# Keys loaded once and queries exchanged on VectorE, in the second attention of an fp32 encoder layer

## The chip, the cores and the metric

The kernel runs on one core of a Trainium2 chip. Its time is the device time of one execution in microseconds (us). Of the kernel before, three runs took 2575.32 to 2576.74 us, with a median of 2575.82 us.

The core has five engines that each run their own instructions in order: TensorE (PE, matmuls), VectorE (DVE), ScalarE (ACT), GpSimd (POOL) and SyncE (SP), which here issues most transfers (DMAs). On-chip memory (SBUF) has 128 partitions; matmuls write to PSUM.

## The reference

One layer of an encoder on 2048 tokens of width 1024, all in float32:

```
h  = rms_norm(x)
z  = h @ W_in            # q_A k_A v_A | q_B k_B v_B | gate_A | gate_B
yA = windowed GQA, |t-s| <= 128, ALiBi, a sink logit per head       (8 heads, 2 kv heads, width 64)
yB = 2-D neighbourhood attention on a 32 x 64 grid of tokens, 8 x 16 keys per query,
     with a learned bias per head and relative position             (8 heads, width 64)
x  = x + (sigmoid(gate_A) * (yA @ Wp_A) + sigmoid(gate_B) * (yB @ Wp_B)) @ W_out
x  = x + relu(rms_norm(x) @ W_up)^2 @ W_down
out = rms_norm(x)
```

## The kernel before, in words

**Precision.** PE multiplies a float32 number as a high and a low part (type fp32r). A product is three matmuls: high by high, high by low, low by high. In the two attentions one operand of 64 rows (a head's width) leaves half of the 128 partitions free, so high and low parts lie on the two halves of the partitions: rows 0 to 63 and rows 64 to 127. One matmul over 128 partitions then gives two of the products, and a second one with the halves of one operand exchanged gives the others.

**Stages.** In the order of PE: the in-projection's first part (0 to about 360 us); the first attention (windowed, class `Unit`, to about 612 us); the second attention (neighbourhood, class `Near`, to about 908 us); the late gates, the projections of the attentions' outputs, and the two MLP products. Both attentions are interleaved with dense matmuls of the in-projection (lines L205 to L207, drawn from a generator by `plain()`), so that PE has work while softmaxes run. Constants (`STEP`, `SCORE`) spread the dense matmuls over the attention's chunks; `in_turn()` ties each of PE's groups behind the one before.

**One unit of the first attention.** 128 queries of four heads. Scores (L846, PE), addition of a bias and maximum (L850, DVE), exponential (L865, ACT), shares, that is the division by the sum (L871, POOL), transposes (L906), the high part (ACT) and low part (DVE) of the transposed shares, the product with v (L931, PE). For the outer keys of a unit, 64-row pieces of v are copied to the tile `ve` (L887, POOL, method `rows`), in one buffer.

**One unit of the second attention.** There are 32 units: 8 heads times 4 column blocks. Scores (L1118): for each of four row groups two matmuls, z = 0 and 1, with the same queries `qb` and with the keys `kb` plain and with halves exchanged. Then bias and maximum (L1125, DVE, a custom operation), exponential (L1138, ACT), the reciprocal of the sum (L1142, DVE), shares (L1145, POOL, `weigh`), transposes (L1157, PE, `turn`), high part `phb` (L1165, ACT), low part `plb` (L1166, DVE), product with v (L1178, PE), sum of the two halves (L1197 and L1198). A loop over "doubles" (half a unit each) makes the transposes of unit n, the scores of unit n + 2 and the loads of unit n + 3.

**Loads of the second attention.** `load_k(h)` loads a head's keys three times over, as `[P, 2, S]`: all 128 rows (1 MB), and the two exchanged halves (0.5 MB each); from the second head on most of them are issued from ACT's queue. `Near.load` loads the queries of a unit (256 KB) and makes its bias: `make_bias_b` (L1070, L1076) loads a table `braw` by DMA and adds the mask to it in three operations on POOL, for three of four column blocks.

**Placement.** The tiles of an attention lie in SBUF in the order of two lists (`ap_` for the first, `bp` for the second). A new tile waits until the old tiles whose bytes it overlaps are done with. The late stage's weights (`graw`) come into the space of the second attention's tiles.

## Time and profile before

| what | value |
|---|---|
| median of 3 runs | 2575.82 us (2575.32 to 2576.74) |
| the profiled execution's own time | 2576.89 us |
| its span, first to last instruction | 2575.1 us |
| granted clock of TensorE, mean | 0.999 |
| busy: PE, DVE, ACT, POOL | 2544.6, 1655.4, 1247.0, 385.3 us |
| transfers | 494.61 MB, 192 GB/s over the span |

The profile's page gives the busy time of each engine. A timeline row gives the start, the length, the engine, the line, the operation with its output and inputs, how many instructions it stands for, and in brackets the engine's idle time just before it and what ended it. A row of waits gives the engine and its line, the releaser, the microseconds in all, how often, and the longest. A row of a stretch gives its length and the busy time of each engine in it.

### The profile page before, as it was taken

Reading aid. Unit: us, or ns where it says so; the run is one execution under the profiler, and the core shown is the slowest. Engines: PE = TensorE matmul, PEld = TensorE weight load, DVE = VectorE, ACT = ScalarE, POOL = GpSimd, SP = SyncE. Lnnn points to the kernel's source line nnn. Section 1 sums busy time; section 2 is a strip of 40 time slices with the busy share of each in tenths; the row PEclk is TensorE's granted clock in tenths of the full one; section 3 lists DMA queues with packets and bytes.
Section 4 is the critical chain, followed back from the end, with each engine's and each line's share of the span. In section 5 each row is a group of like instructions: output and inputs, shape, how many; then the busy total and the mean of one; then the engine's idle time right before and its main releaser. Section 6 shows DMA issues by size and latency. Waiting matters only on the chain.

```text
span 2575.1 us, 34947 instructions
## 1 busy us (share of the span) xinstructions
PE 2544.6 (99%) x12152; PEld 2131.9 (83%) x12152; DVE 1655.4 (64%) x2691; ACT 1247.0 (48%) x2283; POOL 385.3 (15%) x622
## 2 busy tenths in 40 slices
PE   8999999999999999999999999999999999999998
PEld 6888888888899888888888888888888888888887
DVE  8776657765565576565568767865666534554766
ACT  5344347776666654443335554554444322323454
POOL 1000126665666400000000000100000000000010
PEclk9999999999999999999999999999999999999999
DMA  5667486577898647576447656844428725444555
GB/s 181 200 165 202 134 263 170 130 194 191 227 245 215 200 149 261 184 229 184 122 161 252 236 199 219 304 160 163 147 111 315 273 103 188 144 156 155 187 194 174
DMA packets 350225, 494.61 MB, mean 192 GB/s; under 512 B 29000, under 2 KB 180808, under 8 KB 347872
## 3 DMA queue, kind: packets, MB, share of 16 engines
q1 hardware_dynamic: 343312, 465.90, 57.2%
q10 hardware_dynamic: 6736, 26.48, 3.4%
q8 instruction: 96, 1.57, 0.3%
q14 instruction: 81, 0.66, 0.1%
HBM read 332.83 MB, written 159.45 MB: 191 GB/s over the span
## 4 chain that ended last, share of the span: by engine, by line
PE 86%; DMA 2%; DVE 1%; POOL 1%; issue 0%; ACT 0%; POOLq 0%; ACTq 0%; DVEq 0%
PE b L318 16%; PE b L319 16%; PE b L320 16%; PE mm L205 5%; PE mm L207 5%; PE mm L206 5%; PE pt L205 2%; PE pt L206 2%; PE pt L207 2%; PE av L1178 2%; PE pt L1157 2%; PE s L1118 2%; PE av L931 1%; PE s L846 1%; PE pt L906 1%; PE zb L318 1%
## 5 line engine op out<-in xcount | busy, mean ns | idle before, releaser
L319 PE MATMUL b<-dwh,dah 128*128 128x512 f32 x896 | 348.9, 389 | 0.0
L320 PE MATMUL b<-dwh,dah 128*128 128x512 f32 x896 | 347.9, 389 | 0.0
L318 PE MATMUL b<-dwh,dah 128*128 128x512 f32 x896 | 339.9, 389 | 0.0
L314 ACT CAST dah<-da 128x1024 fp32r<-128x1024 f32 (+1 forms) x128 | 120.7, 944 | 367.7 <-PE b L320 244.2
L315 DVE TENSOR_TENSOR dah<-da,dah 128x1024 fp32r<-128x1024 f32 (+1 forms) x128 | 139.6, 1090 | 224.9 <-ACT dah L314 222.0
L319 PE MATMUL b<-ubh,uwhlb 128*128 128x512 f32 x592 | 230.5, 389 | 0.0
L318 PE MATMUL b<-ubh,uwhlb 128*128 128x512 f32 x592 | 230.4, 390 | 0.0
L320 PE MATMUL b<-ubh,uwhlb 128*128 128x512 f32 x592 | 229.4, 389 | 0.0
L318 PEld LDWEIGHTS b<-dwh,dah 128*128 128x128 f32 x896 | 168.3, 188 | 34.9
L319 PEld LDWEIGHTS b<-dwh,dah 128*128 128x128 f32 x896 | 168.3, 188 | 34.8
L320 PEld LDWEIGHTS b<-dwh,dah 128*128 128x128 f32 x896 | 168.3, 188 | 34.8
L318 PE MATMUL zb<-zh,zwhl 128*128 128x512 f32 x476 | 186.8, 394 | 5.0 <-DVE zc L309 1.7
L319 PE MATMUL zb<-zh,zwhl 128*128 128x512 f32 x476 | 186.0, 391 | 0.0
L320 PE MATMUL zb<-zh,zwhl 128*128 128x512 f32 x476 | 183.1, 391 | 1.8 <-DVE zwhl L315 1.8
L309 DVE TENSOR_TENSOR uc<-b,uc 128x512 f32<-128x512 f32 x160 | 109.1, 689 | 103.7 <-PE b L320 102.8
L205 PE MATMUL mm<-hT,whl 128*128 128x512 f32 x416 | 167.9, 404 | 0.7 <-DVE zc L309 0.7
L207 PE MATMUL mm<-hT,whl 128*128 128x512 f32 x416 | 163.5, 393 | 0.0
L206 PE MATMUL mm<-hT,whl 128*128 128x512 f32 x416 | 163.2, 392 | 0.0
L1876 POOL TENSOR_TENSOR st<-st,power 128x1 f32<-128x1 f32 x16 | 13.3, 841 | 925.2 <-DVE st L1875 925.2
L318 PEld LDWEIGHTS b<-ubh,uwhlb 128*128 128x128 f32 x592 | 111.2, 188 | 23.4 <-issue 0.4
L319 PEld LDWEIGHTS b<-ubh,uwhlb 128*128 128x128 f32 x592 | 111.2, 188 | 23.0
L320 PEld LDWEIGHTS b<-ubh,uwhlb 128*128 128x128 f32 x592 | 111.2, 188 | 23.0
(348 smaller groups left out, 6054.4 us busy)
## 6 DMA issues: line engine op xcount, KB each, us to landing
at<-uc SPq DMA_DIRECT2D x224, 256.0 KB
da<-at SPq DMA_DIRECT2D x96, 512.0 KB
dw<-in_w_down_dram SPq DMA_DIRECT2D x160, 256.0 KB
uraw<-in_w_up_dram SPq DMA_DIRECT2D x32, 1024.0 KB
zraw<-in_w_in_dram SPq DMA_DIRECT2D x16, 1024.0 KB
z<-zg SPq DMA_DIRECT2D x64, 256.0 KB
raw<-in_w_in_dram SPq DMA_DIRECT2D x26, 512.0 KB
zg<-zc SPq DMA_DIRECT2D x32, 256.0 KB
```

The source lines that it names most:

```text
L205: PE.matmul(ps, lh, rh, start=first, stop=False)
L206: PE.matmul(ps, lh, rl, start=False, stop=False)
L207: return PE.matmul(ps, ll, rh, start=False, stop=last).ins
L309: return eng.tensor_tensor(out=out, in0=a, in1=b, op=op).ins
L314: casts.append(A.copy(hi, src).ins)
L315: return eng.tensor_tensor(out=lo, in0=src, in1=hi.bitcast(F32), op=ALU.subtract).ins
L318: PE.matmul(ps, lh, rh, start=first, stop=False, skip_group_check=True)
L319: PE.matmul(ps, lh, rl, start=False, stop=False, skip_group_check=True)
L320: PE.matmul(ps, ll, rh, start=False, stop=last, skip_group_check=True)
L1118: ins = PE.matmul(ps[:, :n], self.q[:, i, :], kv[:, z, B_R0[i] // 4 : (B_R0[i] + B_NR[i]) // 4, 4 * B_C0[j] : 4 * (B_C0[j] + w)], start=z ...
L1157: ins = PE.transpose(pt[:kp, at + (i - i0) * P : at + (i - i0 + 1) * P], self.s[i][:, rr : rr + kp], ident).ins
L1178: issued[0] = PE.matmul(po[:, i0 * P : (i0 + ni) * P], self.v[:kp, c, :], src[:kp, o : o + ni * P], start=pair == x == z == 0, stop=(c == ...
```

## The change

Four things change together.

1. `load_k` loads a head's keys once, as `[P, S]`, in two halves along the tokens, both from SP. The tile of the queries has two versions, z = 0 plain and z = 1 with halves exchanged. The scores' two matmuls use the same keys, and the two versions of the queries.
2. The exchanged version is made on DVE by two copies of 64 rows (`swap`), except for units 0 and 1, which get it by two more DMAs each. The queries are loaded a unit earlier (`load_q`, unit n + 4 instead of n + 3).
3. The operations that make a bias are tied behind the last share that was written, or, ahead of any share of the second attention, behind chosen copies of `ve`; a unit's bias is loaded and made after `weigh` instead of first in the unit.
4. `ve` gets two buffers, and the copies for unit n + 1 are written behind the shares in unit n. In the placement, `qraw` goes to the end of its list, and `qb2` behind `biasl`.

```
-    ap_ = pools(s_a, "left", ("ka1", "va1", "qraw", "qa", "sta", "sa", "ya", "ph", "pl", "biasa1", "byhead", "ve"), "a")
+    ap_ = pools(s_a, "left", ("ka1", "va1", "qa", "sta", "sa", "ya", "ph", "pl", "biasa1", "byhead", "ve", "qraw"), "a")
...
         def rows(self):
-            self.ve = T(ap_, [P, 2, P], F32R, "ve", 1)
+            self.ve = T(ap_, [P, 2, P], F32R, "ve", 2)
...
-                        G.tensor_copy(out=self.ve[half, c // 2], in_=rows)
+                        last = G.tensor_copy(out=self.ve[half, c // 2], in_=rows).ins
+            copied_rows.append(last)
...
-        if c == "outer":
-            x.rows()
...
+        if c == "outer" and n + 1 < len(units):
+            with tc.issue_after(shares[-1]):
+                units[n + 1].rows()
...
-    bp = pools(s_b, "right", ("masks", "kb0", "qb0", "braw0", "biass0", "stb", "biass1", "qb1", "qb2", "braw1", "biasl", "kb1"), "b")
+    bp = pools(s_b, "right", ("masks", "kb0", "qb0", "braw0", "biass0", "stb", "biass1", "qb1", "braw1", "biasl", "qb2", "kb1"), "b")
...
-            G.tensor_tensor(out=out.rearrange("p (q x r) -> p q x r", x=w, r=4),
+            first_bias.append(copied_rows[min(22 + len(first_bias), 31)])
+            with tc.issue_after(last_share[0] or first_bias[-1]):
+                G.tensor_tensor(out=out.rearrange("p (q x r) -> p q x r", x=w, r=4),
...
     def load_k(h):
-        kbs[h] = k = T(bp, [P, 2, S], F32R, f"kb{h % 2}", 1)
-        kd = ks_b[h // 2][h % 2]
-        for n, (dst, src) in enumerate(((k[:, 0], kd), (k[0:64, 1], kd[64:128]), (k[64:128, 1], kd[0:64]))):
-            (SY if h == 0 or h == 1 and n == 0 else A).dma_start(dst.bitcast(F32), src)
+        kbs[h] = k = T(bp, [P, S], F32R, f"kb{h % 2}", 1)
+        for n in range(2):
+            at = slice(n * (S // 2), (n + 1) * (S // 2))
+            SY.dma_start(k[:, at].bitcast(F32), ks_b[h // 2][h % 2][:, at])
             yield
...
-            self.q = T(bp, [P, 4, P], F32R, f"qb{self.n % 3}", 1)
-            SY.dma_start(self.q.bitcast(F32), qs_b[self.h // 2][self.h % 2][:, :, self.j])
             return self.bias
+
+        def load_q(self, both=False):
+            self.q = T(bp, [P, 2, 4, P], F32R, f"qb{self.n % 3}", 1)
+            SY.dma_start(self.q[:, 0].bitcast(F32), qs_b[self.h // 2][self.h % 2][:, :, self.j])
+            for a in (0, 64) if both else ():
+                SY.dma_start(self.q[a : a + 64, 1].bitcast(F32), qs_b[self.h // 2][self.h % 2][64 - a : 128 - a, :, self.j])
+
+        def swap(self):
+            q = self.q
+            for a in (0, 64):
+                V.tensor_copy(out=q[a : a + 64, 1], in_=q[64 - a : 128 - a, 0].bitcast(F32))
...
-                    ins = PE.matmul(ps[:, :n], self.q[:, i, :],
-                                    kv[:, z, B_R0[i] // 4 : (B_R0[i] + B_NR[i]) // 4, 4 * B_C0[j] : 4 * (B_C0[j] + w)],
+                    ins = PE.matmul(ps[:, :n], self.q[:, z, i, :],
+                                    kv[:, B_R0[i] // 4 : (B_R0[i] + B_NR[i]) // 4, 4 * B_C0[j] : 4 * (B_C0[j] + w)],
...
-                G.tensor_scalar(s[i][:, :n], s[i][:, :n], ri[:, i : i + 1], 1.0, ALU.mult, ALU.mult)
+                last_share[0] = G.tensor_scalar(s[i][:, :n], s[i][:, :n], ri[:, i : i + 1], 1.0, ALU.mult, ALU.mult).ins
...
         if p == 0:
-            if n + 3 < len(units):
-                bias = units[n + 3].load(bias)
+            if n + 4 < len(units):
+                units[n + 4].load_q()
...
+        with behind_parts_b():
+            for u in (2, 3) if at == 0 else (n + 3,) if p == 0 and n + 3 < len(units) else ():
+                units[u].swap()
         if weighed:
             with behind_parts_b():
                 y, us = weighed.pop(0)
                 y.weigh(us)
+        if p == 0 and n + 3 < len(units):
+            bias = units[n + 3].load(bias)
```

The order of POOL's work at the end of the second attention's first units, before (`whl` is a low part of the dense matmuls' weights, `biass` and `biasl` are biases, `sb` shares):

```order
L1145 TENSOR_SCALAR sb_745_6700<-sb_745_6700,stb_6635 128x384
L182 TENSOR_TENSOR whl_6816<-raw_6503,whl_6816 128x1024
L1076 TENSOR_TENSOR biass_800_7067<-braw_801_7068,masks_6383 128x288
L1076 TENSOR_TENSOR biass_800_7067<-braw_801_7068,masks_6383 128x384
L1076 TENSOR_TENSOR biass_800_7067<-braw_801_7068,masks_6383 128x288
L1145 TENSOR_SCALAR sb_756_6746<-sb_756_6746,stb_6742 128x288
L1145 TENSOR_SCALAR sb_757_6751<-sb_757_6751,stb_6742 128x384
L1145 TENSOR_SCALAR sb_762_6798<-sb_762_6798,stb_6742 128x384
L1145 TENSOR_SCALAR sb_763_6803<-sb_763_6803,stb_6742 128x288
```

and with the change, from the shares of unit 0 to the bias behind the shares of unit 1:

```order
L1160 TENSOR_SCALAR sb_699_6429<-sb_699_6429,stb_6410 128x288
L1082 TENSOR_TENSOR biasl_6441<-braw_701_6442,masks_6383 128x384
L1082 TENSOR_TENSOR biasl_6441<-braw_701_6442,masks_6383 128x512
L1082 TENSOR_TENSOR biasl_6441<-braw_701_6442,masks_6383 128x384
L887 COPY ve_6199<-va_294_2980 64x128 x2
L1160 TENSOR_SCALAR sb_706_6457<-sb_706_6457,stb_6453 128x288
L1160 TENSOR_SCALAR sb_707_6462<-sb_707_6462,stb_6453 128x384
L1160 TENSOR_SCALAR sb_708_6467<-sb_708_6467,stb_6453 128x384
L1160 TENSOR_SCALAR sb_709_6472<-sb_709_6472,stb_6453 128x288
L1082 TENSOR_TENSOR biass_732_6611<-braw_733_6612,masks_6383 128x288
L1082 TENSOR_TENSOR biass_732_6611<-braw_733_6612,masks_6383 128x384
L1082 TENSOR_TENSOR biass_732_6611<-braw_733_6612,masks_6383 128x288
```

A bias that stood ahead of a unit's shares stands behind the shares of the unit before.

DVE at the first double of the second attention, with the change (`qb` are the queries, the lines L1114 the exchange; L1181 is the low part, L1140 the scores' bias and maximum):

```order
L1181 TENSOR_TENSOR plb_6503<-pt_6497,phb_6502 96x512
L1114 CAST qb_702_6447<-qb_702_6447 64x512 x2
L1114 CAST qb_710_6484<-qb_710_6484 64x512 x2
L444 TENSOR_TENSOR z_6531<-mm_6530,z_6531 128x8x64
L1181 TENSOR_TENSOR plb_6551<-pt_6543,phb_6550 96x512
L1140 ISA sb_725_6566,stb_6562<-s_6563,biasl_6441 128x384
L1140 ISA stb_6562 128x1
```

Before, only the low part, the same `z` and the scores' rows stood here. Four copies have come between two low parts; later units have two copies each, also between a low part and the next scores.

SP at the turn to the late stage, before:

```order
L1104 DMA vb_1231_9851<-vs_b_96 128x4x256
L554 DMA graw_10276<-in_w_in_dram 128x4x512
L554 DMA graw_10278<-in_w_in_dram 128x4x512
L1335 DMA graw_10286<-h1d_97 128x512
L1335 DMA graw_10286<-h1d_98 128x512
```

and with the change:

```order
L1119 DMA vb_1248_10021<-vs_b_96 96x4x256
L178 DMA y_b_108<-yb_6382 256x1x128
L292 DMA gt_11046<-in_norm_mlp_dram 32x32
L554 DMA graw_10332<-in_w_in_dram 128x4x512
L554 DMA graw_10334<-in_w_in_dram 128x4x512
L1358 DMA graw_10342<-h1d_97 128x512
```

The late weights' loads have moved behind the loads of the last unit's rows of v. The first of them waited for PE's scores of unit 30 before; with the change it waits for the reciprocal on DVE and a share on POOL of unit 31.

More of the change, by code (lines that the diff above doesn't have):

```diff
@@ L1014, in encoder_layer @@
     chunks = [(n, c) for n, x in enumerate(units) for c in x.groups()]
+    copied_rows = []
+    units[0].rows()
     behind, weighed, scored, begin = [], [], 0, given
@@ L1049, in encoder_layer @@
     s_b = ExitStack()
-    bp = pools(s_b, "right", ("masks", "kb0", "qb0", "braw0", "biass0", "stb", "biass1", "qb1", "qb2", "braw1", "biasl", "kb1"), "b")
+    bp = pools(s_b, "right", ("masks", "kb0", "qb0", "braw0", "biass0", "stb", "biass1", "qb1", "braw1", "biasl", "qb2", "kb1"), "b")
     bp.update(pools(s_b, "left", ("sb0", "sb1", "sb2", "vb0", "vb1", "vb2", "phb", "plb", "yb"), "b"))
     boff, bstart, btotal = bias_layout()
-    last_exp, last_parts, n_raw, n_short = [None], [None], [0], [0]
+    last_exp, last_parts, n_raw, n_short, last_share, first_bias = [None], [None], [0], [0], [None], []
     yb = T(bp, [P, BT], F32, "yb", 1)
@@ L1075, in make_bias_b @@
             out, mask, rows = t[:, o : o + n], masks[:, jstart[jt] + o : jstart[jt] + o + n], raw[:, at : at + n]
-            G.tensor_tensor(out=out.rearrange("p (q x r) -> p q x r", x=w, r=4),
-                            in0=rows.rearrange("p (q r x) -> p q x r", x=w, r=4),
-                            in1=mask.rearrange("p (q x r) -> p q x r", x=w, r=4), op=ALU.add)
+            first_bias.append(copied_rows[min(22 + len(first_bias), 31)])
+            with tc.issue_after(last_share[0] or first_bias[-1]):
+                G.tensor_tensor(out=out.rearrange("p (q x r) -> p q x r", x=w, r=4),
+                                in0=rows.rearrange("p (q r x) -> p q x r", x=w, r=4),
+                                in1=mask.rearrange("p (q x r) -> p q x r", x=w, r=4), op=ALU.add)
         return t
     def load_k(h):
-        kbs[h] = k = T(bp, [P, 2, S], F32R, f"kb{h % 2}", 1)
-        kd = ks_b[h // 2][h % 2]
-        for n, (dst, src) in enumerate(((k[:, 0], kd), (k[0:64, 1], kd[64:128]), (k[64:128, 1], kd[0:64]))):
-            (SY if h == 0 or h == 1 and n == 0 else A).dma_start(dst.bitcast(F32), src)
+        kbs[h] = k = T(bp, [P, S], F32R, f"kb{h % 2}", 1)
+        for n in range(2):
+            at = slice(n * (S // 2), (n + 1) * (S // 2))
+            SY.dma_start(k[:, at].bitcast(F32), ks_b[h // 2][h % 2][:, at])
             yield
@@ L1111, in score @@
             mx, nm, sm, ri = (self.st[:, n, :] for n in range(4))
-            kv = self.k.rearrange("p z (q f) -> p z q f", q=8)
+            kv = self.k.rearrange("p (q f) -> p q f", q=8)
             s = self.s
@@ L1229, in encoder_layer @@
         bias = units[n].load(bias)
+        units[n].load_q(True)
     for n in range(2):
@@ L1238, in encoder_layer @@
             bias = units[2].load(bias)
+            units[2].load_q()
             keys = load_k(1)
             next(keys)
+    units[3].load_q()
     doubles = [(n, p) for n in range(len(units)) for p in (0, 2)]
```

## The prediction

> **What bounds the kernel now.** I read the page first, then the stretches around the two attentions, then the waits of TensorE (PE), then the timelines of the engines that PE waited for. The page's first part:
>
> ```profile
> span 2575.1 us, 34947 instructions
> PE 2544.6 (99%) x12152; PEld 2131.9 (83%) x12152; DVE 1655.4 (64%) x2691; ACT 1247.0 (48%) x2283; POOL 385.3 (15%) x622
> ```
>
> PE is busy all but 30.5 us, and the change takes no matmul away. So it can win only idle time of PE, and only in the stages whose code it touches, from 340 to 960 us. The view by stretches (length; busy time of PE, its loads, DVE, ACT, POOL; clock; DMA share; GB/s):
>
> ```profile
> 560.00:618.00 58.00, 55.71 (x328) 48.30 (x329) 34.24 (x93) 36.86 (x97) 38.63 (x68) 1.00 0.52 132
> 618.00:660.00 42.00, 37.56 (x224) 32.16 (x223) 24.49 (x63) 24.72 (x62) 22.03 (x25) 1.00 0.95 261
> 660.00:900.00 240.00, 240.00 (x1516) 216.57 (x1515) 138.74 (x375) 162.79 (x405) 142.41 (x168) 1.00 0.82 220
> 900.00:960.00 60.00, 59.58 (x277) 49.46 (x276) 45.28 (x60) 32.17 (x47) 1.34 (x1) 1.00 0.49 154
> ```
>
> The clock is full everywhere. PE lost 2.29 us in 560 to 618 and 4.44 us in 618 to 660, where the DMA engines are 95% busy, and nothing in the 240 us behind, the steady part of the second attention. All that can be won lies in the turn from the first attention to the second. What PE waited for from 480 to 960 (engine, line, releaser: us, times, longest):
>
> ```profile
> PE pt L1157 <- POOL sb L1145: 2.0, 1, 2.0
> PE av L931 <- POOL ve L887: 1.7, 1, 1.7
> PE av L1178 <- DMA vb<-vs_b: 1.3, 1, 1.3
> PE av L1178 <- DVE plb L1166: 0.9, 2, 0.7
> PE av L931 <- POOL sb L1145: 0.6, 1, 0.6
> ```
>
> These six stalls are 6.5 us. The view counts a stall from the modelled end of the matmul before, 0.39 us after its start, though two dense matmuls start 0.23 us apart. So each costs 0.16 us more: 6.5 + 6 x 0.16 = 7.4 us. Behind them POOL's and DVE's timelines (start, length, engine, work, idle before and its releaser):
>
> ```profile
> 561.96 3.04 POOL L1076 TENSOR_TENSOR biass<-braw,masks 128x288 f32<-128x288 f32 x3 [3.58 <-DMA braw<-tab]
> ...
> 566.99 1.31 POOL L887 CAST ve<-va 64x128 fp32r<-64x128 f32 x4
> 618.75 3.90 POOL L1076 TENSOR_TENSOR biasl<-braw,masks 128x384 f32<-128x384 f32 x3 [2.90 <-DMA braw<-tab]
> 650.37 3.02 POOL L1076 TENSOR_TENSOR biass<-braw,masks 128x288 f32<-128x288 f32 x3 [5.66 <-DMA braw<-tab]
> 653.35 2.11 POOL L1145 TENSOR_SCALAR sb<-sb,stb 128x288 f32<-128x288 f32 x4
> 611.11 0.18 DVE L1142 RECIPROCAL stb<-stb 128x4 f32<-128x4 f32 x1 [1.86 <-ACT sb L1138]
> 620.00 0.56 DVE L1125 CUSTOM_DVE_ANT_0 sb<-s,biasl 128x384 f32<-128x384 f32 x1 [4.86 <-POOL biasl L1076]
> ```
>
> One pattern stands in three of them. POOL runs in order; a bias of the second attention stands ahead of shares or of rows of v, and waits for its table (`braw`). At 650.37 POOL has waited 5.66 us, then makes the bias for 3.0 us, and only then the shares (653.35) that PE's transposes need. At 561.96 the same holds up the copies `ve` (566.99), and at 618.75 the bias itself is late for DVE, whose low parts `plb` queue behind. PE's rows there:
>
> ```profile
> 568.35 0.50 PE L931 MATMUL av<-ph,ve 128*128 128x256 f32 x2 [1.72 <-POOL ve L887]
> 611.93 0.36 PE L931 MATMUL av<-ph,ve 128*128 128x256 f32 x1 [0.57 <-POOL sb L1145]
> 621.82 0.39 PE L1178 MATMUL av<-plb,vb 96*128 96x256 f32 x1 [0.74 <-DVE plb L1166]
> 635.66 0.39 PE L1178 MATMUL av<-plb,vb 128*128 128x256 f32 x1 [0.21 <-DVE plb L1166]
> 646.54 0.36 PE L1178 MATMUL av<-phb,vb 128*128 128x256 f32 x1 [1.26 <-DMA vb<-vs_b]
> 632.11 0.93 PE L1157 MATMUL pt<-ident,sb 128*128 128x128 f32 x7
> 640.64 1.50 PE L1157 MATMUL pt<-ident,sb 128*128 128x128 f32 x7
> 653.92 1.43 PE L1157 MATMUL pt<-ident,sb 128*96 128x128 f32 x7 [1.97 <-POOL sb L1145]
> ```
>
> Seven transposes take 0.93 us when nothing holds them, 1.50 and 1.43 where POOL makes the shares while PE reads them. That is 1.07 us by these rows, of which I count 0.7, since the ends are modelled. In all 7.4 + 0.7 = 8.1 us can be won, no more.
>
> **The change part by part.** *Biases behind shares, loaded after `weigh`.* No instruction more or less. In the new order the bias that stood ahead of the shares at 653.35 stands behind them, and the shares of units 0 and 1 run before the next bias too. This removes the 2.13 us at 653.92 (1.97 + 0.16), the two long groups (0.7) and, since the bias for units 2 and 3 now comes right after the shares of unit 0, the 0.90 at 621.82. The reciprocal at 611.11, which waited 1.86 us for the exponentials and held up a low part (611.93, 0.73 us), stands behind other work now: gone too. What is late next: a bias now waits with only the next unit's shares behind it. Not all moves. The first bias of the second attention is still ahead of shares, and of the second only one of three operations; at 561.96 that leaves about one operation (3.04 / 3 = 1.0 us) of the 3.04 ahead of `ve`, so I leave 0.5 of the 1.88 us.
>
> *`ve` in two buffers.* It removes no copy, and POOL's waits for PE before them are covered by its slack. Its own worth is in the 1.88 us already counted.
>
> *Keys once.* The DMAs of the stretch 610 to 660:
>
> ```profile
> kb<-ks_b ACTq DMA_DIRECT2D x4, 512.0 KB
> kb<-ks_b SPq DMA_DIRECT2D x1, 1024.0 KB
> kb<-ks_b ACTq DMA_DIRECT2D x1, 1024.0 KB
> ```
>
> That is 4 MB for two heads; now 2 MB. At the 261 GB/s of this stretch 2 MB less are 8.0 us of 42. So the rows of v that landed 1.42 us late (646.54) and the tables land earlier; a stall of 1.42 us is covered several times over. From ACT's queue 20 issues vanish, two of which stood around a cast at 634 to 635 (0.37 us at 635.66). SP gets two key loads a head instead, in order with its others; the queries go out one unit earlier on it, into a buffer whose scores were done a unit before, so that nothing behind them on SP is held up; units 0 and 1 cost four more half loads of 128 KB, in the 52% busy stretch before 618. In the steady part this wins nothing, because PE is idle 0.00 us there.
>
> *The exchange on VectorE.* Sixty copies of 64x512 from SBUF to SBUF, two a unit. No row of before is such a copy. The nearest, with the scores' tile (times of one; first and last start) and the wait of DVE that is longest:
>
> ```profile
> L1198 DVE TENSOR_TENSOR yb<-av,yb 64x512 f32<-64x512 f32 x32 | 21.9, 684 | 0.7 <-ACT yb L1197 0.2
> L269 DVE TENSOR_SCALAR xr<-xr,st 128x1024 f32<-128x1024 f32 x16 | 12.0, 752 | 13.5 <-DMA x2d<-xr 12.4 <-POOL st L260 0.7
> L182 POOL TENSOR_TENSOR whl<-raw,whl 128x1024 fp32r<-128x1024 f32 x24 | 57.7, 2404 | 25.5 <-ACT whl L181 25.5
> L1118 PE MATMUL s<-kb,qb x256: 291/342/480, 587.2 to 885.4; 128*128 128x384 f32 x64, 128*128 128x288 f32 x32, 128*128 128x512 f32 x32
> DVE plb L1166 <- ACT phb L1165: 72.6, 41, 5.2
> ```
>
> Above, 0.684 us: same shape, two sources. Below, half of 0.752, 0.38 us: one source in SBUF, as here. I take 0.4, the row it resembles: 60 x 0.4 = 24 us on DVE, at most 41. From 660 to 900 DVE is idle 240 - 138.74 = 101 us, and the 32 units (x32 in the first row) are scored in 885 - 587 = 298 us, 9.3 each: 26 of them, with 3.9 us idle a unit, against 0.8 (1.4 at most) added. Queued behind a copy on DVE are the next low part and the next addition of scores and bias, which PE needs half a unit (4.6 us) later. So I cost it at nothing in the steady part. Four copies come at once at the first double (1.6, at most 2.8 us), where DVE was idle 4.86 us (620.00); but the low parts behind them are near their due time there, and a weight cast of 2.40 us on POOL now stands ahead of unit 2's shares: 0.9 us for both, between 0 and 2.4.
>
> [...]
>
> *The first attention's start.* Its queries' raw tile moves to the end of its pools, and its first two scores come some ten dense matmuls later in PE's order, next to the other two: filled from both sides by dense work, I cost it at nothing (at most 1 us, the length of two scores behind two others).
>
> *The turn to the late stage.* The buffers that now hold the last unit's work overlap those of the late weights (`graw`), so their loads wait for unit 31's reciprocal and shares instead of unit 30's scores. SP, POOL, DVE and PE there:
>
> ```profile
> 891.54 2.10 POOL L1145 TENSOR_SCALAR sb<-sb,stb 128x288 f32<-128x288 f32 x4 [5.04 <-DVE stb L1142]
> 877.01 0.94 SPq L554 DMA_DIRECT2D graw<-in_w_in_dram x2
> 906.74 1.21 DVE L309 TENSOR_TENSOR gS<-graw,graw 128x1024 f32<-128x1024 f32 x1
> 916.58 1.22 DVE L315 TENSOR_TENSOR gwhl<-gS,gwhl 128x1024 fp32r<-128x1024 f32 x1
> 918.28 0.62 PE L318 MATMUL pt<-gh,gwhl 128*128 128x512 f32 x2
> ```
>
> Issue moves from 877.0 to about 892.5, and SP's own queue behind it (stores of y, rows of the late stage) by as much. The 4 MB (two loads of 1 MB, eight of 256 KB) take 16 us at 261 GB/s: 908.5, 1.8 us after the first use at 906.7; PE's first late matmul starts 0.5 us after its weights are done (917.8), which leaves 1.3. At the stretch's 154 GB/s it would be far more; but nothing else loads then, so 0.7 us, between 0 and 9.
>
> *Sum.* 8.1 - 0.5 - 0.9 - 0.7 = 6.0 us. The profiled execution took 2576.89 us (span 2575.1), 1.07 above the median of 2575.82. So 2570.9 for it, and 2569.8 for the median.
>
> **Rivals.** *The waits only move (no change).* What speaks for it: DMA stays 82 to 95% busy, and POOL is as full as before. If what hangs on transfers stays, the 1.88 at 568, 0.90 at 621 and 1.42 at 646, the change wins 8.1 - 4.2 - 0.9 - 0.7 = 2.3 us: 2573.5. Against it: 2 MB less in the worst 42 us, and the shares no longer stand behind those waits.
>
> *VectorE becomes late in every unit (slower).* Its place is the pair of copies between two low parts. If each copy waits for the POOL operation that runs (0.5 us of a share, 1.0 of a bias, 2.40 of a weight cast; POOL is busy 142.41 of 240, so 0.59 x about 0.55 us left of one = 0.3), the pair costs 2 x (0.69 + 0.3) = 2.0 us of the 3.9 idle, and the low parts behind slip by it. It decides from 0.20 us of PE a unit on (6.0 / 30), and shows as slower from (6.0 + 5.2) / 30 = 0.37. At 0.45 us a unit it is 13.5 us: 2575.82 - 6.0 + 13.5 = 2583.3. Against it: DVE is not what PE waits for there, it waits itself, 72.6 us in all, for ACT's casts ahead of the low parts.
>
> *The late weights miss their use (no change).* At 154 to 261 GB/s the 4 MB take 16 to 27 us; in the middle, 21, PE stalls 6.5 us, and 2575.82 - 6.7 + 6.5 = 2575.6. Against it: DMA engines freed from keys and queries.
>
> *The change does nothing.* Key traffic is hidden work where PE has no idle time; then the gain is that of the order on POOL alone. This is inside the first rival.
>
> **How the numbers follow.** A difference under 0.2%, 5.15 us, can't be told from no change here. Forecast as worked out 0.54; waits that only move 0.24; late weights 0.08; VectorE late 0.14. The forecast's own range is 2567.2 (8.1 won, 0.5 more elsewhere) to 2571.5; about an eighth of it lies above 2575.82 - 5.15 = 2570.67. So faster is 0.54 x 7/8 = 0.47, same 0.07 + 0.24 + 0.08 = 0.39, slower 0.14. The whole range goes up to 2577.0, which takes in both cases of no change and leaves out the slow one.
>
> **What would show it.** In the changed profile: no wait of PE's transposes L1172 for POOL's shares, the `ve` wait under 0.6 us, POOL's waits for `braw` with nothing of PE behind them; DMA share in 618 to 660 well under 0.95; copies of 64x512 on DVE at 0.35 to 0.45 us; 660 to 900 with PE full. A row of PE waiting for DVE's scores or copies in most units, or a PE wait at the first late matmul over 1.5 us, would make the forecast wrong, as would copies over 1 us.

## The result

The changed kernel takes 2568.1 us (median of 7 runs, 2566.39 to 2571.45), the kernel before 2576.9 us (median of 7 runs beside it, 2575.32 to 2580.57). The ratio is 0.9965 with a 95% interval of 0.9954 to 0.9977: 5.9 to 11.9 us less, 8.8 by the medians. It is faster, by more than the 0.2% that can be told from no change. The profiled execution has a span of 2565.9 us against 2575.1.

The page after, and the stretches that the prediction showed of before (length; busy time of PE, its loads, DVE, ACT, POOL; clock; DMA share; GB/s):

```profile
span 2565.9 us, 34914 instructions
PE 2542.1 (99%) x12152; PEld 2130.9 (83%) x12152; DVE 1690.9 (66%) x2751; ACT 1247.9 (49%) x2283; POOL 384.5 (15%) x622
```

```profile
560.00:618.00 58.00, 58.00 (x345) 50.72 (x345) 40.31 (x102) 38.14 (x99) 38.37 (x64) 1.00 0.54 148
618.00:660.00 42.00, 41.76 (x262) 37.20 (x261) 32.75 (x81) 29.84 (x73) 19.31 (x24) 1.00 0.76 205
660.00:900.00 240.00, 240.00 (x1509) 215.90 (x1508) 161.53 (x410) 160.34 (x395) 145.19 (x169) 1.00 0.69 198
900.00:960.00 60.00, 59.58 (x267) 49.14 (x266) 46.65 (x61) 32.06 (x46) 0.00 (x0) 1.00 0.50 154
```

The turn between the attentions is full: PE's idle time from 560 to 660 went from 6.73 to 0.24 us, and the DMA share from 618 to 660 from 0.95 to 0.76. The steady part stayed full with 23 us more work on DVE. What PE waits for from 340 to 960 us now (times as in the waits of before):

```profile
PE s L846 <- POOL qa L828: 1.0, 1, 1.0
PE zb L318 <- DVE zc L309: 0.6, 1, 0.6
PE s L318 <- DVE gc L309: 0.4, 1, 0.4
PE s L846 <- DVE sta L850: 0.4, 1, 0.4
PE pt L1172 <- POOL sb L1160: 0.2, 1, 0.2
```

None of the six stalls of before is left. Two new ones stand at the start of the first attention (L846). POOL's timeline at the places that the prediction showed:

```profile
561.80 0.95 POOL L1082 TENSOR_TENSOR biass<-braw,masks 128x288 f32<-128x288 f32 x1 [3.45 <-DMA braw<-tab]
...
565.30 1.28 POOL L887 CAST ve<-va 64x128 fp32r<-64x128 f32 x4
...
625.71 2.50 POOL L1160 TENSOR_SCALAR sb<-sb,stb 128x384 f32<-128x384 f32 x4 [12.65 <-DVE stb L1157]
628.16 3.94 POOL L1082 TENSOR_TENSOR biasl<-braw,masks 128x384 f32<-128x384 f32 x3
635.11 2.49 POOL L1160 TENSOR_SCALAR sb<-sb,stb 128x384 f32<-128x384 f32 x4 [3.02 <-DVE stb L1157]
```

At 561.80 POOL still waits 3.45 us for a table, but only one of the bias's three operations follows, and the copies `ve` are done at 566.58 instead of 568.30. From there on no bias waits for a table at all, and the shares wait for DVE's reciprocals: POOL is early, not late.

**Where the time went, by stage.** The dense matmuls of the in-projection (L205 to L207, 1248 records in every trace here) come in one order in all kernels, so that the time between two of them compares a stage. I read four lengths from the start times in each trace: from the start of the last in-projection matmul ahead of the attentions to the 61st dense one (the start), to the 421st (the first attention), to the 721st (the turn, 541 to 689 us in before), and to the 1141st (the steady part).

| kernel | start | first attention | turn | steady part | median of its runs |
|---|---|---|---|---|---|
| before | 17.65 | 164.82 | 147.97 | 205.01 | 2576.6 to 2578.2 by chip |
| the change | 18.74 | 164.52 | 139.47 | 205.03 | 2568.1 |

The turn gained 8.50 us and the start lost 1.09. Of what is left of the 9.2 us between the two spans, 1.2 us lie ahead of the attentions, in code that the change doesn't touch: the last in-projection matmul started at 358.91 in before and at 357.73 after. In the traces below it starts anywhere from 356.2 to 358.9, so that is a difference between executions. The first attention and what follows the steady part are 0.3 us shorter each. I compare the kernels by stages for this reason, and by their timed runs for the verdicts.

### The profile page after: what moved, and what is told of

Its sections match the earlier page's. It is cut to its first block, busy times and chain, and to the rows that moved or that the text cites. A ratio compares the mean times of both kernels' runs of the same rounds, so it can differ in the third digit from the quotient of the medians.

```text
span 2565.9 us, 34914 instructions
## 1 busy us (share of the span) xinstructions
PE 2542.1 (99%) x12152; PEld 2130.9 (83%) x12152; DVE 1690.9 (66%) x2751; ACT 1247.9 (49%) x2283; POOL 384.5 (15%) x622
## 4 chain that ended last, share of the span: by engine, by line
PE 93%; DVE 3%; DMA 2%; issue 1%; ACT 1%; SPq 1%; POOL 0%; POOLq 0%; DVEq 0%; ACTq 0%
PE b L318 16%; PE b L320 16%; PE b L319 16%; PE mm L205 5%; PE mm L207 5%; PE mm L206 5%; PE zb L320 3%; PE zb L318 3%; PE zb L319 3%; PE pt L205 2%; PE pt L206 2%; PE pt L207 2%; PE av L1193 2%; PE pt L1172 2%; PE s L1133 2%; PE av L932 1%
## 5 line engine op out<-in xcount | busy, mean ns | idle before, releaser
L205 PE MATMUL mm<-hT,whl 128*128 128x512 f32 x416 | 167.6, 403 | 0.0
L207 PE MATMUL mm<-hT,whl 128*128 128x512 f32 x416 | 163.4, 393 | 0.0
```

The lines of the kernel that those rows point to most:

```text
L205: PE.matmul(ps, lh, rh, start=first, stop=False)
L207: return PE.matmul(ps, ll, rh, start=False, stop=last).ins
```

## The experiments

Theories: *O*, the order on POOL held PE up, and the ties took that away. *T*, the transfers were too slow, and loading keys once took that away. *R*, the one buffer of rows of v made POOL late. *Placement*, where `qraw` and `qb2` lie decides when queries can be loaded. For the copies on DVE: *slack*, only DVE's free time counts, against the second rival, in which each copy waits for the POOL operation that runs.

The stage lengths of all kernels, to which the sections refer:

| kernel | what it is | start | turn | steady part | median us | ratio to before, 95% interval |
|---|---|---|---|---|---|---|
| p1_biases | before + ties | 16.68 | 141.55 | 205.01 | 2572.6 | 0.9980 (0.9971 to 0.9989) |
| p2_rows | before + two buffers for rows of v | 16.66 | 150.86 | 205.01 | 2576.5 | 0.9991 (0.9982 to 0.9999) |
| p3_keys | before + keys once, `qb2` moved | 17.81 | 156.16 | 205.01 | 2584.4 | 1.0027 (1.0016 to 1.0037) |
| p4_keys | before + keys once | 16.68 | 154.57 | 205.01 | 2579.9 | 1.0011 (1.0002 to 1.0020) |
| u1_qraw | the change, `qraw` not moved | 18.34 | 145.17 | 205.03 | 2572.1 | 0.9978 (0.9969 to 0.9986) |
| u2_keys | the change, keys as before | 18.86 | 143.44 | 205.01 | 2572.8 | 0.9982 (0.9973 to 0.9991) |
| u3_places | the change, neither tile moved | 16.69 | 139.52 | 205.03 | 2566.3 | 0.9957 (0.9943 to 0.9970) |
| u4_rows | u3_places, rows of v as before | 16.67 | 141.17 | 205.02 | 2569.8 | 0.9971 (0.9960 to 0.9981) |
| d2_swaps | the change, copies made twice | 18.95 | 142.73 | 206.95 | 2572.9 | 0.9986 (0.9977 to 0.9995) |
| d3_swaps | the change, copies made three times | 18.01 | 155.37 | 226.72 | 2604.1 | 1.0106 (1.0092 to 1.0120) |
| d6_swaps | the change, copies made six times | 21.68 | 183.10 | 321.48 | 2725.2 | 1.0578 (1.0564 to 1.0593) |
| c3_reduce | the change + four reductions a unit | 18.57 | 142.79 | 207.24 | 2574.7 | 0.9990 (0.9981 to 0.9999) |

### The ties alone

```
+            first_bias.append(copied_rows[min(22 + len(first_bias), 31)])
+            with tc.issue_after(last_share[0] or first_bias[-1]):
                 G.tensor_tensor(out=out..., in0=rows..., in1=mask..., op=ALU.add)
...
-                bias = units[n + 3].load(bias)
+                units[n + 3].load_q()
...
+        if p == 0 and n + 3 < len(units):
+            bias = units[n + 3].load(bias)
```

> The kernel before with one part of the change: the biases tied behind shares, and a unit's bias loaded and made after its exponentials are written; keys, queries, rows of v and placement as before. Theory O (what held PE up was the order on POOL): the stalls at 568, 612, 622 and 654 go, 1.9 + 0.7 + 0.9 + 2.1 + 0.7 = 6.3 us, and the rows of v that land late at 646 (1.4 us) and the low part at 636 (0.4) stay: 6 us faster than before, PE idle in 560 to 660 about 2 us instead of 6.7. Theory T (the transfers were too slow, whatever the order): a bias behind shares still comes late for DVE, at most 2 us faster.

It won 5.2 us by the ratio, and 6.4 in the turn. Its profiled execution lost 0.9 of that in the first attention (the first wait below) and 2.7 behind the steady part. PE's waits from 480 to 960, and the stretch that was fullest of transfers before:

```profile
PE av L932 <- DVE pl L916: 0.9, 1, 0.9
PE av L1184 <- DVE plb L1172: 0.7, 1, 0.7
PE pt L1163 <- DVE plb L1172: 0.6, 1, 0.6
PE s L318 <- DVE gc L309: 0.4, 1, 0.4
PE av L1184 <- ACT phb L1171: 0.2, 1, 0.2
618.00:660.00 42.00, 41.32 (x253) 36.58 (x254) 28.08 (x74) 29.06 (x73) 20.63 (x26) 1.00 0.97 264
```

No wait for POOL and none for the rows of v is left, with the DMA share in 618 to 660 still at 0.97. PE's idle time from 560 to 660 is 1.56 us. Theory O stands: most of the gain is order, and it needs no byte less. The edit also moves a unit's table behind its queries among SP's loads (in before the table that POOL waited for at 650 was issued at 638.47, here the one at that place at 633.50); what that adds to the order on POOL is not separated. What remains is on DVE and not at the two places I named.

### The rows of v alone

```
-            self.ve = T(ap_, [P, 2, P], F32R, "ve", 1)
+            self.ve = T(ap_, [P, 2, P], F32R, "ve", 2)
...
-        if c == "outer":
-            x.rows()
+        if c == "outer" and n + 1 < len(units):
+            with tc.issue_after(shares[-1]):
+                units[n + 1].rows()
```

> The kernel before with one part of the change: two buffers for the rows of v, and the copies for the next unit written behind the shares. Theory O: only the stall at 568 can go, since its bias no longer stands ahead of the copies: 0 to 1.9 us faster. Theory R (the one buffer made POOL late, 64.6 us of waits for PE): POOL runs ahead everywhere and most of the 8.5 us are won.

The timed runs are 2.3 us faster, within an interval that nearly reaches none. In the turn it lost 2.9 us. The stall at 568 is gone, but one other has grown and one is new. Below them the stretch from 618 to 660:

```profile
PE pt L1161 <- POOL sb L1149: 3.3, 1, 3.3
PE s L1122 <- DMA qb<-qs_b: 2.5, 1, 2.5
618.00:660.00 42.00, 38.62 (x221) 33.63 (x220) 22.30 (x59) 23.57 (x59) 19.57 (x24) 0.90 0.92 240
```

POOL ran ahead, and a bias that waits for its table stood ahead of the shares as before; the queries of a unit came late as well. Theory R falls. Its profile is faster only ahead of the turn: 1.0 us in the start (17.65 to 16.66), 1.8 in the in-projection.

Why the turn is longer than before is not in PE's idle time, which is 6.6 us from 560 to 660, against 6.7 before. It is the granted clock, 0.90 in the stretch above, where before and the change have 1.00. The trace has it at one half for 3.4 us from 616.29 and for 6.8 us from 650.42, beside the two long waits. Dense matmuls start 0.43 us apart there, and 0.23 elsewhere. PE works for 9.0 of these 10.2 us, so my estimate of the cost is 9.0 x (1 - 0.23 / 0.43) = 4.2 us, more than the 2.9 that the turn lost. A long wait of PE is paid for twice here.

### Keys once, alone

Two kernels: one with the changed place of `qb2`, one with both places as before. Both leave ties and rows of v as in before. Against the change:

```
-            first_bias.append(copied_rows[min(22 + len(first_bias), 31)])
-            with tc.issue_after(last_share[0] or first_bias[-1]):
-                G.tensor_tensor(out=out..., in0=rows..., in1=mask..., op=ALU.add)
+            G.tensor_tensor(out=out..., in0=rows..., in1=mask..., op=ALU.add)
...
-            self.ve = T(ap_, [P, 2, P], F32R, "ve", 2)
+            self.ve = T(ap_, [P, 2, P], F32R, "ve", 1)
...
+            if n + 3 < len(units):
+                bias = units[n + 3].load(bias)
...
-        if p == 0 and n + 3 < len(units):
-            bias = units[n + 3].load(bias)
```

> The changed kernel without its ties and without the second buffer for rows of v (both as before, and the queries' raw tile placed as before): what is left is keys loaded once and the exchange on VectorE. Theory O: 646 and 636 go (1.8 us), the stalls behind the biases become shorter by what the tables land earlier, 568 and 612 stay: 2 to 4 us faster than before. Theory T: 654, 622, 646, 636 all go with the key traffic, 5.5 us faster, DMA share in 618 to 660 near 0.76.

> The kernel before with keys loaded once and the exchange on DVE alone, with both placements as before; biases not tied, rows of v in one buffer. Its counterpart with the third queries' buffer moved was 6 us slower than before, with 4.0 us of stalls for late queries at 617 to 620 and 6.0 us for shares at 649. Placement theory: the 4.0 us go, since unit 2's queries load early again, and the shares behind a bias that waits for its table stay: about 2 us slower to 2 us faster than before. Theory T (fewer bytes let the tables land in time): the stall at 649 goes too, 4 us or more faster than before.

Both are slower than before, by 6.2 and 2.9 us; every theory expected a gain of the first. The turn of p4_keys, POOL's timeline and PE's longest wait:

```profile
643.66 2.96 POOL L1078 TENSOR_TENSOR biass<-braw,masks 128x288 f32<-128x288 f32 x3 [6.25 <-DMA braw<-tab]
646.60 2.49 POOL L1156 TENSOR_SCALAR sb<-sb,stb 128x384 f32<-128x384 f32 x4
```

```profile
618.00:660.00 42.00, 34.98 (x197) 30.51 (x198) 29.11 (x65) 21.24 (x52) 18.80 (x20) 0.92 0.72 195
PE pt L1168 <- POOL sb L1156: 5.9, 1, 5.9
```

The DMA engines are at 72%, and yet POOL waits 6.25 us for a table with the shares behind it. The bytes weren't what made PE wait: the table's load was issued at 637.50, and its bias began 6.2 us later, where before it took 11.9 (638.47 to 650.37). But that bias now stands one group of shares earlier in POOL's order. In before the two groups of 128x384 run ahead of it, in p4_keys only the first (630.97); PE's 5.9 us are for the second. POOL in before:

```profile
629.95 2.48 POOL L1145 TENSOR_SCALAR sb<-sb,stb 128x384 f32<-128x384 f32 x4 [7.29 <-DVE stb L1142]
...
639.82 2.50 POOL L1145 TENSOR_SCALAR sb<-sb,stb 128x384 f32<-128x384 f32 x4 [1.71 <-DVE stb L1142]
```

So theory T falls as the cause of this stall, and the loss is one of order again. Part of it is the clock once more: at one half for 3.4 us from 567.45 and for 6.8 us from 645.95, an estimated 4.2 us of the 6.6 that the turn lost (in p3_keys 13.7 us at one half, an estimated 4.6). The 4.0 us for queries at 617 to 620 in p3_keys are 0.6 in p4_keys (0.3 of it in the waits for the copies). That is the time that the placement theory gave; the next section shows that its reason, the late load, was the smaller part.

### The change with one or both tiles in their old place

```
-    ap_ = pools(s_a, "left", ("ka1", "va1", "qa", ..., "byhead", "ve", "qraw"), "a")
+    ap_ = pools(s_a, "left", ("ka1", "va1", "qraw", "qa", ..., "byhead", "ve"), "a")
```

and in u3_places also

```
-    bp = pools(s_b, "right", ("masks", ..., "qb1", "braw1", "biasl", "qb2", "kb1"), "b")
+    bp = pools(s_b, "right", ("masks", ..., "qb1", "qb2", "braw1", "biasl", "kb1"), "b")
```

> The changed kernel with the raw queries' tile of the first attention placed as before (third in its list). In the changed profile the first scores waited 1.1 + 0.5 us at 370 for queries whose loads were issued at 362.6 instead of 349. Placement theory: this stall goes and the stall of 0.8 at 360 returns, 0.8 us faster than the change. But in the order the long bias of the second attention moves behind the next unit's shares; if that bias was what gave the 0.9 at 622, 0.1 us net, no difference that can be seen in the times, only at those two places of the profile.

> The changed kernel with both placements as before (raw queries third in the first attention's list, third buffer of queries behind the second in the second's). With the first alone undone, unit 2's queries were loaded at 608.5 instead of 578 and PE waited 3.6 us at 617.5 for their exchange. In the order of this one they go out early again, and the first scores keep their place. Placement theory (that stall was the late load, not the exchange): it is gone, and the 1.6 us at 370 of the change too: as fast as the change or up to 1.5 us faster, 9 to 10 us under before. If the exchange itself held PE up: about 2572, as with the first alone undone.

With `qraw` alone put back, the turn is 5.7 us longer than with the change and the kernel 3 to 4 us slower: both of my expectations of u1_qraw were wrong. With both put back, it is the fastest kernel of this study, 2566.3 us. Its start is 2.05 us shorter than the change's and its turn the same. Against the change itself the timed intervals overlap (0.9943 to 0.9970, 0.9954 to 0.9977); that it is the better one rests on the start alone, where its PE has no wait. And a start can be late for another reason: u1_qraw, which has `qraw` in the same old place, took 18.34 us, since PE waited 1.1 us there for DVE, DVE for POOL, and POOL 9.48 us for a bias table of the first attention.

The stall of u1_qraw was not what I had written. DVE and POOL at that place, the copies' rows of the tile `qb` (shortest, median, longest in ns), and PE's wait:

```profile
611.81 5.68 DVE L1114 CAST qb<-qb 64x512 fp32r<-64x512 f32 x4
```

```profile
609.68 3.92 POOL L1082 TENSOR_TENSOR biasl<-braw,masks 128x384 f32<-128x384 f32 x3
613.55 2.35 POOL L182 TENSOR_TENSOR whl<-raw,whl 128x1024 fp32r<-128x1024 f32 x1
```

```profile
L1114 DVE CAST qb<-qb x60: 420/422/4375, 611.8 to 869.8; 64x512 fp32r<-64x512 f32 x60
PE s L1133 <- DVE qb L1114: 3.6, 1, 3.6
```

By the trace the queries were there, since DVE began the first copy at 611.81. It lasted 4.375 us instead of 0.42 and ended at 616.18, 0.28 us after POOL's weight cast (613.55 + 2.35 = 615.90). It ran across the end of one bias operation, the whole next one, and the cast. The four copies came while POOL worked without a gap (609.68 to 615.90), and the first of them ended only behind the last of its operations. In u3_places POOL's long bias waits until 613.69 and the copies pass almost at once (the longest there takes 0.53 us). So by this trace the place of `qb2` worked through the order on POOL more than through the load. The same in p3_keys: one copy of 4.806 us. Behind the 3.6 us wait the clock was at one half for 3.4 us, an estimated 1.6 us of the 5.7.

### Keys as before in the changed kernel

```
-        kbs[h] = k = T(bp, [P, S], F32R, f"kb{h % 2}", 1)
+        kbs[h] = k = T(bp, [P, 2, S], F32R, f"kb{h % 2}", 1)
...
-        with behind_parts_b():
-            for u in (2, 3) if at == 0 else (n + 3,) if p == 0 and n + 3 < len(units) else ():
-                units[u].swap()
```

> The changed kernel with keys and queries as before (keys loaded twice over, no exchange on DVE, queries one unit later); ties, rows of v and the raw queries' place as changed. Theory O (order on POOL made the gain, key traffic little): within 2 us of the change, 7 to 9 us faster than before, DMA share in 618 to 660 again about 0.95. Theory T: the rows of v and the tables land late again, PE stalls of 3 us or more between 610 and 660, at most 5 us faster than before.

The edit takes the whole part back: the keys in three loads, twice over (2 MB a head instead of 1), the queries a unit later and `qb2` in its old place. It is 4.6 us faster than before and 4 to 5 us slower than the change, nearly all of it in the turn (143.44 against 139.47). Here theory T came nearer than theory O:

```profile
618.00:660.00 42.00, 39.28 (x237) 34.08 (x237) 25.73 (x65) 26.68 (x67) 18.89 (x23) 1.00 0.98 273
```

The DMA engines are at 98% again, and PE's 2.7 us of idle time there go to rows of v that land late (1.2 us in the waits), and to casts and low parts. So with the ties and the second buffer in place the keys are worth about 4 us; without them they cost 7 (p4_keys), of which an estimated 4.2 are clock. The parts do not add: alone they change the turn by -6.4, +2.9 and +6.6 us, together by -8.5.

### The second buffer for rows of v in the best version

```
-            self.ve = T(ap_, [P, 2, P], F32R, "ve", 2)
+            self.ve = T(ap_, [P, 2, P], F32R, "ve", 1)
...
+        if c == "outer":
+            x.rows()
...
-        if c == "outer" and n + 1 < len(units):
-            with tc.issue_after(shares[-1]):
-                units[n + 1].rows()
```

> The best version so far (the change with both placements as before) with the rows of v as before: one buffer, copied in the unit's own outer part. Theory O (ties decide, the second buffer only lets the copies go ahead of the biases): the stall at 568 stays away because the first bias is tied behind copies; within 1.5 us of the best version, 9 to 11 us faster than before. Theory R: without the second buffer POOL waits for PE again (64.6 us in before) and shares come late: 2 us or more slower than the best version.

By the medians 3.5 us slower than u3_places, by the turn 1.65. The intervals of the two overlap. The stall at 568 stayed away, as theory O said. What came is one wait for the copies at 613 (1.84 us between the starts of two matmuls, 1.6 in the waits): one copy of 2.490 us there stood beside a weight cast of POOL's (2.54 us from 610.51), as in u1_qraw. Theory R's waits for POOL did not come back into the turn.

### More copies

```
-            for a in (0, 64):
+            for a in (0, 64) * 3:
                 V.tensor_copy(out=q[a : a + 64, 1], in_=q[64 - a : 128 - a, 0].bitcast(F32))
```

(2 and 6 in the other two.)

> The changed kernel with each exchange made twice (four copies a unit). Three times cost 36 us, at 89% of DVE's time. If the loss begins where a burst of copies no longer fits between two low parts, two more copies (0.84 us a unit) cost little: 0 to 5 us slower than the change. If it is in proportion to the copies: 18 us slower.

> The changed kernel with each exchange made three times (six copies a unit instead of two). In the changed profile a free copy took 0.42 us, eight of sixty waited for a POOL operation, and DVE was idle 240 - 161.5 = 78.5 us in 660 to 900, 3.0 us a unit. Four more copies are 1.7 us a unit. Slack theory: fits, PE full in 660 to 900, the same time as the change within 1 us or so; at the first double four copies become twelve (5 us), which can cost up to 2 us there. [...]

> The changed kernel with each exchange made six times (twelve copies a unit). Ten more copies are 4.2 us a unit against 3.0 us of idle DVE: DVE becomes the bound from 620 to 880. Slack theory: PE stalls 1.2 to 2 us a unit, 36 to 60 us slower than the change. If DVE's idle time were not what decides, the loss would be smaller or already there with three.

Twice costs 4.8 us, three times 36, six times 157. The slack theory said none for three and 36 to 60 for six; it is wrong by a long way. In d3_swaps, from 660 to 900 us, with the longest waits of PE from 600 on:

```profile
660.00:900.00 240.00, 225.44 (x1367) 197.09 (x1365) 213.83 (x489) 144.27 (x366) 152.43 (x159) 0.99 0.64 174
PE pt L1172 <- DVE plb L1181: 6.9, 14, 1.6
PE av L1193 <- DVE plb L1181: 6.8, 10, 2.0
PE s L1133 <- DVE qb L1114: 5.1, 1, 5.1
```

DVE is 89% busy: 52 more than in the change, of which four free copies of 0.42 us for 26 units are only 44. PE waits for low parts 24 times. What happens between the copies and POOL:

```profile
746.44 2.82 DVE L1114 CAST qb<-qb 64x512 fp32r<-64x512 f32 x4
```

```profile
746.50 3.21 POOL L1160 TENSOR_SCALAR sb<-sb,stb 128x384 f32<-128x384 f32 x4 [7.02 <-DVE stb L1157]
```

Four copies took 2.82 us instead of 1.69, and four shares beside them 3.21 instead of 2.50 (625.71 above). Both sides pay in these rows, the copies 1.13 us and the shares 0.71. Of the 180 copies 79 took over 0.47 us, 27 us more in all than free ones; the shares of 128x384 have a mean of 721 ns against 589 in the change:

```profile
L1160 POOL TENSOR_SCALAR sb<-sb,stb 128x384 f32<-128x384 f32 x62 | 44.4, 721 | 88.3 <-DVE stb L1157 73.0 <-PE s L1133 8.1 <-PE pt L1172 7.2
```

Not all of the 36 and 157 us is waiting. In d3_swaps the clock was at one half in four spells of 17.1 us in all, from 618 to 724, which costs an estimated 7 us; in d6_swaps it was so for 123 us, an estimated 46. In d6_swaps PE's longest waits are for the copies themselves (64.4 us, 26 times), not for low parts (35.1).

### The same time on DVE in reductions

```
+            for n in range(4):
+                junk = T(bp, [P, 1], F32, "junkb", 1)
+                V.tensor_reduce(out=junk[0:64], in_=q[0:64, 0, 0:2].rearrange("p i q -> p (i q)").bitcast(F32), op=ALU.max,
+                                axis=mybir.AxisListType.X)
```

> The changed kernel with four reductions of 64x256 from SBUF added to each unit's exchange, in place of the four added copies of the run with six copies. A reduction reads one tile and should take about 0.42 us as a free copy does; 79 of 180 copies there waited for a POOL operation (27 us in all), and POOL's operations for them. [...] Slack theory (only DVE's time counts, whatever the operation): about the same loss as with six copies, less the 27 us spread over DVE: 25 us or more.

6.6 us slower than the change, against 36 with four copies more. The reductions' rows, the stretch, and the shares beside them (busy us, mean ns):

```profile
L1117 DVE TENSOR_REDUCE junkb<-qb x120: 379/411/427, 615.0 to 875.7; 64x1 f32<-64x256 f32 x120
```

```profile
660.00:900.00 240.00, 238.96 (x1501) 214.11 (x1500) 196.88 (x511) 159.73 (x397) 146.31 (x170) 1.00 0.67 189
```

```profile
L1164 POOL TENSOR_SCALAR sb<-sb,stb 128x384 f32<-128x384 f32 x62 | 36.3, 592 | 74.6 <-DVE stb L1161 64.2 <-PE pt L1176 10.4
```

Not one of 120 reductions was held up (longest 427 ns), and POOL's shares kept their 592 ns. As many operations of nearly the same free length cost a fifth of what the copies cost. What sets the two apart in these traces is that copies and POOL's operations held each other up (79 of 180 copies over 0.47 us, shares of 721 ns) and reductions and POOL's operations did not (none of 120 over 0.427 us, shares of 592 ns), with two reservations. The scores wait for the copies of a unit and for no reduction; the waits above say that this was the smaller part (5.1 us once, against 13.7 for low parts). And the estimated 7 us of slow clock in d3_swaps come on top of its waits, while c3_reduce has none in the attentions.

## Why the prediction was right, and where it was off

**The range, the sign and the place were right.** 2568.1 us lies in 2567.2 to 2577.0, faster with the largest chance, by 8.8 us where 6.0 were forecast. The gain came where the prediction put it, in the turn (8.5 us by the traces); the steady part gave and took 0.0 us, the late stage 0.3, and the start gave back 1.1. That the sum came this near is partly luck: three charges of 2.1 us in all came to 0.2 at most, and a term put at nothing cost 1.1.

**The recoverable 8.1 us, "no more": right within 0.4.** The turn gained 8.5.

**"I leave 0.5 of the 1.88 us" (the first bias): not needed.** Of the bias at 561.80 one operation of 0.95 us stands ahead, and POOL's copies end 1.7 us earlier; PE waited for nothing there.

**"0.9 us for both" (four copies at the first double, a weight cast ahead of shares): too much.** The four copies took 1.89 us at 612.8 and met the rest of a weight cast once, for 0.15 us. PE lost nothing to either, and 0.2 us in all on shares at 636.

**"0.7 us" for the late weights: not needed.** SP, DVE and PE there:

```profile
884.80 0.94 SPq L554 DMA_DIRECT2D graw<-in_w_in_dram x2
897.88 1.21 DVE L309 TENSOR_TENSOR gS<-graw,graw 128x1024 f32<-128x1024 f32 x1
909.41 0.62 PE L318 MATMUL pt<-gh,gwhl 128*128 128x512 f32 x2
```

The loads were issued 7.8 us later by the clock, 16.7 later against PE's work, where 15.5 were forecast. The first use and PE's first late matmul both came 8.9 us earlier than before, which is the whole shift, so what the first use needs had landed within 13.1 us of the first issue. I had let it wait for all 4 MB, at 261 GB/s, 16 us.

**"I cost it at nothing" (the first attention's start): wrong by 1.1 us.**

```profile
362.63 1.91 SPq L824 DMA_DIRECT2D qraw<-qs_a x3
369.53 0.61 POOL L828 CAST qa<-qraw 128x512 fp32r<-128x512 f32 x1 [4.62 <-DMA qraw<-qs_a]
370.19 0.69 PE L846 MATMUL s<-ka,qa 128*128 128x160 f32 x4 [0.98 <-POOL qa L828]
```

Behind the end of its list `qraw` lies on space that is free later: its first loads went out at 362.63 (349.09 before), POOL waited 4.62 us for them, and PE 1.0 us, and 0.4 us more for the four scores in a row. u3_places, where `qraw` lies as before, has neither. The price is nearer 2 us than 1.1. A start without a wait of PE takes 16.66 to 16.69 us (five traces, all with `qraw` as before), 2.05 less than the change's, and before itself had a wait of 0.65 us for DVE at 359.95 that the change's trace lacks. Five of the six traces with `qraw` moved wait for POOL's casts of the queries here, none of the eight others does.

**The reasons, step by step.** That order held PE up, and not the bytes, is shown (ties alone -6.4 us in the turn, at a DMA share of 0.97 against 0.95); that it was POOL's order and not also SP's rests on the rows of POOL at the three stalls. That fewer key bytes cover "a stall of 1.42 us several times over" is right only behind the ties and the buffer: u2_keys against the change, 4.0 us in the turn. Alone the key part lost 6.6, since a bias moved ahead of one more group of shares and the clock was at one half for 10.2 us beside its two long waits; the prediction's first rival, which let the waits move, was nearer there than its forecast. The prediction counted the second buffer's worth inside the 1.88 us; alone it was -2.9, behind the ties 1.65 (not settled by the timed runs).

**The copies.** A free copy took 0.42 us, near the lower bound of 0.38, and the trace shows the wait of the second rival: seven of sixty copies in the change waited for POOL, 5.5 us in all. The copies (shortest, median, longest in ns), and one of the seven, DVE and POOL:

```profile
L1114 DVE CAST qb<-qb x60: 419/422/1605, 612.8 to 865.1; 64x512 fp32r<-64x512 f32 x60
711.64 2.04 DVE L1114 CAST qb<-qb 64x512 fp32r<-64x512 f32 x2
```

```profile
710.52 2.44 POOL L182 TENSOR_TENSOR whl<-raw,whl 128x1024 fp32r<-128x1024 f32 x1
```

The second copy took 0.42 us, so the first ended at 713.25, 0.29 us after the weight cast. The rival let a copy wait for the rest of one operation, 0.3 us; the copy of 4.375 us in u1_qraw waited across the rest of one and two whole ones. Four of the seven took 1.5 to 1.6 us, and by the prediction's own sign, copies over 1 us, the forecast should have failed; PE lost nothing to them. It held because these waits were few: two units in ten, 0.15 to 1.2 us each, at places with as much room. The prediction's argument for it, that DVE is idle 3.9 us a unit, was the wrong measure: with 0.84 us more a unit PE lost 1.9 us in the steady part, with 1.7 us more 21.7, while DVE still had 26 us of idle time in 660 to 900. PE's waits there are for low parts, so the time from a cast on ACT to the product that needs its low part is the likelier measure; how much room it has was not measured.

## What to carry to other kernels

Look at what stands ahead of the urgent work on a quiet in-order engine: POOL was busy 15% of the time, and biases that waited for a transfer ahead of shares cost PE most of the 8.5 us (6.4 came back with the ties alone). An operation that is moved to another engine for "free" should be tried at twice its dose: here two copies a unit were free in the steady part, four cost 5 us and six 36. Read the granted clock beside PE's idle time: in four kernels here (p2_rows, p3_keys, p4_keys, u1_qraw) long waits cost an estimated 1.6 to 4.6 us of slow matmuls on top. Parts of such a change don't add, and a tile's place in SBUF can be worth as much as the idea: the same edits were 2572 or 2566 us with one tile in one place or another.

## What the runs showed of the hardware that was not expected

- Copies of 64x512 on DVE from SBUF to SBUF waited out a POOL operation that ran: all 307 over 0.47 us in ten traces ended 0.27 to 0.29 us after the end of one (free ones took 0.42 us). Where POOL's operations followed each other without a gap, a copy was passed over: in u1_qraw one took 4.375 us, across the rest of one POOL operation and two whole ones, in p3_keys one took 4.806. In d3_swaps, from 746.44, four copies took 2.82 us instead of 1.69, beside four shares that took 3.21 instead of 2.50.
- It worked the other way too: POOL's shares of 128x384 took 721 ns beside six copies a unit (d3_swaps), 589 beside two (the change). The reductions of c3_reduce, about as long as a free copy, took 379 to 427 ns beside the same POOL work, and the shares 592.
- In these traces the granted clock of TensorE was at one half beside every wait of PE of 2.43 us or more behind 340 us: for 3.4 and 6.8 us in p2_rows (waits of 2.5 and 3.3 us) and in p4_keys (2.4 and 5.9), for 3.4 us in u1_qraw (3.6). In d3_swaps (17.1 us in four spells) it was so also beside waits of 2.0 us or less that stood close together. The longest wait of before, 1.97 us, brought none. Dense matmuls started 0.43 us apart at that clock in p2_rows, and 0.23 elsewhere.
- The execution's first 358 us, which no kernel here changes, ended anywhere between 356.2 and 358.9 us in the traces, as much as a third of what the change won.
